# Dilated attention in near blocks and residues modulo 4, the two parts joined through DRAM

## The chip, the core and the metric

The kernel runs on one core of a Trainium2 chip. The metric is the device time of one execution in microseconds (us). The kernel before takes 1123.94 us, the median of three runs (1122.03 to 1125.61). The engines are TensorE (PE: matmuls and transposes; its weight loads are listed as PEld), VectorE (DVE), ScalarE (ACT), GpSimdE (POOL, which here issues most loads of the attention) and SyncE (SP, which issues the other DMAs).

## The reference, cut to what matters

One decoder layer on a sequence of 1024 tokens, width 1024. A projection of 10 pieces feeds two branches: attention with 8 heads of 64, and a gated recurrence. Gates merge them, and a last matmul and a norm end the layer. The change touches the attention alone. It is a mixture of three causal patterns, (window, dilation) = (128, 1), (512, 4) and (2048, 16):

```python
DILATED_PATTERNS = ((128, 1), (512, 4), (2048, 16))
...
    s = jnp.einsum('bdhnqe,bdhnke->bdhnqk', qs, ks) * (E ** -0.5) + bias[None, None, :, None]
    s = jnp.where(mask, s, NEG_INF)
    m = jnp.max(s, axis=-1, keepdims=True)
    p = jnp.exp(s - m)
    den = jnp.sum(p, axis=-1, keepdims=True)
    o = jnp.einsum('bdhnqk,bdhnke->bdhnqe', p, vs) / den
    lse = (m + jnp.log(den))[..., 0]
...
    w = jax.nn.softmax(jnp.stack(lses, 0), axis=0)
    return jnp.einsum('gbsh,gbshe->bshe', w, jnp.stack(outs, 0))
```

The three outputs are weighted with their denominators, so the mixture is a single softmax in which a key at distance delta counts as often as there are patterns that reach it: 0, 1, 2 or 3 times. A query sees every key up to a distance of 128, and beyond that only keys whose distance is a multiple of 4.

## The kernel before

All weights are split into a high and a low part of type float32r, and most products are three matmuls (high by high, low by high, high by low; mm3, lines 241 to 243). The projections form a **stream** of steps of 12 matmuls of 512 columns each. A step is prepared ahead of its product: DMA of the raw weights, ACT casts the high part (w_hi, line 248), DVE subtracts (w_lo, line 226, a helper that also makes ptl). Results leave the three banks m0 to m2 through ACT copies (line 329) and DVE additions (line 276).

The order of PE's instructions is written out by hand. In the attention stage pieces of attention stand between steps of the stream: `fill(amount)` runs as many quarters of a step as an amount times a rate comes to, so that the stream is spread over the stage. The other engines' orders come from a scheduler and are then fixed; each engine runs its queue in order.

Attention before, for each head h:

- load_head and load_half load queries (qp: both halves of the 128 partitions hold high and low parts), keys (k1, k2) and the biases by distance (toep, 1024 offsets); load_value loads values (vq), all on POOL's queue.
- score(h, i) makes the row of queries 128i to 128i+127 against all keys up to there, 128(i+1) wide, in chunks of at most 512 columns: two matmuls a chunk (lines 923 and 924), one DVE operation that adds the bias and takes the extreme (line 926), exp with its sum on ACT (line 929), a reciprocal (line 930) and the scaling (line 931). That is 36 blocks of 128x128 a head.
- turn(h, j, m, ...) transposes three or four blocks of a pair of rows on PE (line 941), and ACT and DVE split them (pth line 945, ptl).
- value(h, j, m, ...) multiplies them with the values (line 956), mostly 256 columns at a time, into one of two halves of a bank; at the end of a pair of rows the result goes out (lines 961 to 963).

The blocks of a row that no pattern needs in full (far keys at distances that are not multiples of 4) are computed and masked by a bias of -1e30.

Of the kernel before, what the change touches and what calls it, by code (L numbers as in the profile page):

```python
# [32 lines left out]
TOEP = 1152  # L33
# [6 lines left out]
def _consts():  # L40
    z = np.arange(TOEP)
    delta = z - (P - 1)
# [7 lines left out]
    for window, dilation in PATTERNS:  # L50
        count += (delta >= 0) & (delta <= window) & (delta % dilation == 0)
# [16 lines left out]
ATT_W = (2.6, 1.4, 0.9, 0.7)  # L68
# [111 lines left out]
def hybrid_layer(ctx: ExitStack, tc: tile.TileContext, x, w_ada, b_ada, w_in, w_branch_a, w_branch_b, w_out,  # L180
# [38 lines left out]
    vq_d = dram.tile([NH // 2, P, 8, 2, P], F32, name="vq_d")  # L219
# [222 lines left out]
    def ev_v(p, wait=2):  # L442
        def ev(src, th, psum):
            t = as_ct(src, psum)

            def turn():
# [3 lines left out]
                for n in (0, 2):  # L450
                    vs = ctile(F32R).rearrange("p (a h e) -> p a h e", a=2, h=2)
                    got = pt[:, n:n + 2].rearrange("p a (h e) -> p a h e", h=2)
                    nc.scalar.copy(vs[:, :, :, 0:E], got)
                    sub(vs[:, :, :, E:P], got, vs[:, :, :, 0:E])
                    nc.sync.dma_start(vq_d[p][:, 4 * th + n:4 * th + n + 2], vs.bitcast(F32))
                    last_v[p] = vs
# [61 lines left out]
    with ExitStack() as st:  # L518
# [184 lines left out]
        def bias_add(b):  # L703
            sl = slice(384 * b, 384 * b + 384)
            nc.vector.tensor_tensor(lc[:, sl], pbs[b], lc[:, sl], ALU.add)
            if b == 2:
                nc.gpsimd.dma_start(toep_d, lc)
# [79 lines left out]
        bias_row(2)  # L787
        bias_add(2)
# [79 lines left out]

    with ExitStack() as at:
# [4 lines left out]
        po2 = psO.tile([P, 2, 256], F32, name="po2")  # L874
        heads = {}

        def load_head(h):
            p = h // 2
            if p > 0:
                stream.need(f"qk{p}")  # L880
            while turned.get(("v", p)) != 2:
                stream.step()
            qp, k1, k2 = ([ap1.tile([P, 512], F32R, name=f"{n}{c}") for c in range(2)] for n in ("qp", "k1", "k2"))
            toep = ap1.tile([P, S], F32, name="toep")
            heads[h] = qp, k1, k2, toep, [None, None]
            load_half(h, 0)
            if h == 0:
                load_half(h, 1)
            load_value(h, 0)

        def load_half(h, c):


            qp, k1, k2, toep, _ = heads[h]
            if h == 0 and c == 1:
                got = last_v[0][:, 0, 0, 0:1].bitcast(F32)
                for t in (qp[1], k1[1], k2[1]):
                    nc.gpsimd.tensor_copy(t[:, 0:1], got)
                nc.gpsimd.tensor_copy(toep[:, 512:513], got)
            nc.gpsimd.dma_start(toep[:, half_of(c)],  # L900
                                bass.AP(tensor=toep_d.tensor, offset=toep_d.offset + h * TOEP + 512 * c,
                                        ap=[[1, P], [1, 512]]))
            p, r = h // 2, slice(E * (h % 2), E * (h % 2) + E)
            for dst, n in ((qp, 4 * p), (k1, 4 * p + 2), (k2, 4 * p + 3)):
                for hh in range(2):
                    nc.gpsimd.dma_start(dst[c][E * hh:E * hh + E],
                                        qk_d[n + hh if dst is qp else n][r, half_of(c)].bitcast(F32R))

        def load_value(h, n):
            vq = heads[h][4][n] = ap2.tile([P, 4, P], F32R, name="vq", bufs=3)  # L910
            nc.gpsimd.dma_start(vq, vq_d[h // 2][:, 4 * n:4 * n + 4, h % 2].bitcast(F32R))

        def score(h, i):
            qp, k1, k2, toep, _ = heads[h]
            kw = P * (i + 1)
            s = ap2.tile([P, (768, 1024)[i // 2 % 2]], F32, name=f"s{i // 2 % 2}")
            st2 = ap2.tile([P, 4], F32, name="st2", bufs=8)
            prev = 3.0e38
            for ks in range(0, kw, 512):
                w = min(512, kw - ks)  # L920
                ps = psS.tile([P, 512], F32, name="pss")
                q = qp[i // 4][:, i % 4 * P:i % 4 * P + P]
                nc.tensor.matmul(ps[:, :w], q, k1[ks // 512][:, :w], start=True, stop=False)  # L923
                nc.tensor.matmul(ps[:, :w], q, k2[ks // 512][:, :w], start=False, stop=True)  # L924
                x0, a = kw - ks - w, ks // 512
                nc.vector.tensor_tensor_reduce(s[:, ks:ks + w], ps[:, :w], toep[:, x0:x0 + w][:, ::-1], -1.0,  # L926
                                               prev, ALU.add, ALU.min, st2[:, a:a + 1])
                prev = st2[:, a:a + 1]
            nc.scalar.activation(s[:, :kw], s[:, :kw], AF.Exp, bias=prev, scale=-1.0, accum_out=st2[:, 2:3])  # L929
            nc.vector.reciprocal(st2[:, 3:4], st2[:, 2:3])  # L930
            nc.vector.tensor_scalar(s[:, :kw], s[:, :kw], st2[:, 3:4], None, ALU.mult)
            return s

        def turn(h, j, m, pn):
            pt = pools["t"].tile([P, 4, P], F32, name="pt").rearrange("p a b -> p (a b)")
            for kk in range(2):
                kt = 2 * m + kk
                for b in range(2):
                    if kt <= 2 * j + b:
                        c0 = kk * 256 + (b * P if kt <= 2 * j else 0)  # L940
                        nc.tensor.transpose(pt[:, c0:c0 + P], pn[b][:, kt * P:(kt + 1) * P], ident)  # L941
            w = 512 if m < j else 384
# [6 lines left out]
        def value(h, j, m, parts):  # L949
            vq, hh = heads[h][4], h % 2  # L950
            po = po2[:, j % 2]
            for kk in range(2):
                kt = 2 * m + kk
                c0, n = kk * 256, (256 if kt <= 2 * j else P)
                for a, src in enumerate(parts):
                    nc.tensor.matmul(po[:, 256 - n:256], vq[kt // 4][:, kt % 4], src[:, c0:c0 + n],  # L956
                                     start=kt == 0 and a == 0, stop=kt == 2 * j + 1 and a == 1)
            if m == j:
                t1 = ap1.tile([E, 256], F32, name="t1")
                oa = ap2.tile([E, 256], F32, name="oa")  # L960
                nc.scalar.copy(t1, po[E:2 * E])
                nc.vector.tensor_tensor(oa, po[0:E], t1, ALU.add)
                nc.sync.dma_start(oa_d[h // 2][E * hh:E * hh + E, 256 * j:256 * j + 256], oa)

        items = [(h, j) for h in range(NH) for j in range(4)]
        rows = {}

        def begin(n):

            if n < len(items):  # L970
                h, j = items[n]
                rows[n] = []
                for i in (2 * j, 2 * j + 1):
                    rows[n].append(score(h, i))
                    if i == 1:
                        if h > 0:
                            load_half(h, 1)
                        load_value(h, 1)
                    if i == 7 and h + 1 < NH:
                        load_head(h + 1)  # L980
                    yield
# [3 lines left out]
        def run_late(keep):  # L985
            while len(late) > keep:
                value(*late.pop(0))

        load_head(0)
        first = begin(0)  # L990
# [510 lines left out]
```

## Time and profile before

| | |
|---|---|
| median of the runs | 1123.94 us |
| the profiled execution's own time | 1122.96 us |
| its span | 1121.1 us |
| PE, DVE, ACT, POOL busy | 1095.0, 806.8, 555.2, 124.6 us |
| attention stage, on the span | 95 to 436 us |
| granted PE clock in it | 1.00 |
| mean DMA rate over the span | 169 GB/s |

The span runs from the first to the last instruction of the program; the time has 1.9 us more around it. In rows of groups, a line of the kernel, the engine, the operation and "output<-inputs" come first, then the shapes and the count, then busy us, mean ns of one, and the idle time of the engine ahead of them with what ended it. In a timeline the first two numbers are the start in the span and the duration, both in us. Durations of overlapping matmuls contain each other.

### The profile page before, as it was taken

What the parts mean: (1) busy time and instruction counts of PE and PEld (TensorE: products, weight loads), DVE (VectorE), ACT (ScalarE), POOL (GpSimd) and SP (SyncE); (2) the same over time, 40 slices, a digit from 0 to 9 for tenths busy, and PEclk for the clock granted to TensorE, in tenths of its full rate; (3) what the DMA queues carried; (4) which work ended last, traced back from release to release, by engine and by line L of the source; (5) the groups of instructions that cost most, each with busy time, mean ns of one, the idle gap of its engine ahead of it and who ended that gap; (6) DMA issues with size and microseconds to landing.
All of it is one profiled execution on the core that took longest, in us unless ns stands there. A gap on an engine that the chain in (4) does not pass through costs nothing.

```text
span 1121.1 us, 21828 instructions
## 1 busy us (share of the span) xinstructions
PE 1095.0 (98%) x8302; PEld 905.4 (81%) x8302; DVE 806.8 (72%) x1607; ACT 555.2 (50%) x1144; POOL 124.6 (11%) x207
## 2 busy tenths in 40 slices
PE   8999999999999999999999999989999999999997
PEld 6687888888888888778887788878887888887886
DVE  5587888878777876844879788887977772869053
ACT  5565656687555555622455554545554442334021
POOL 1112203203212201100000000000010012000000
PEclk9999999999999999999999999999999999999999
DMA  9849657736636625756625354353534389854052
GB/s 311 261 128 251 172 173 200 176 95 181 162 102 169 153 66 171 248 174 201 217 86 180 119 175 138 127 160 95 184 122 159 131 266 343 258 193 141 14 188 75
DMA packets 161608, 189.54 MB, mean 169 GB/s; under 512 B 11440, under 2 KB 107824, under 8 KB 161504
## 3 DMA queue, kind: packets, MB, share of 16 engines
q1 hardware_dynamic: 140080, 153.95, 42.6%
q0 software_dynamic: 21024, 33.60, 12.2%
q8 instruction: 65, 1.06, 0.4%
q10 hardware_dynamic: 400, 0.61, 0.2%
q14 instruction: 39, 0.32, 0.1%
HBM read 129.36 MB, written 58.76 MB: 168 GB/s over the span
## 4 chain that ended last, share of the span: by engine, by line
PE 78%; DVE 8%; issue 7%; DMA 3%; ACT 2%; POOL 1%; POOLq 0%; DVEq 0%; ACTq 0%
PE m L241 15%; PE m L243 15%; PE m L242 15%; PE pq L241 4%; PE pq L242 4%; PE pq L243 4%; PE po L956 2%; PE pt L941 2%; PE pp L1122 2%; PE pss L924 1%; PE pss L923 1%; DVE w_lo L226 1%; PE pou L1218 1%; PE pm L669 1%; PE pm L672 1%
## 5 line engine op out<-in xcount | busy, mean ns | idle before, releaser
L226 DVE TENSOR_TENSOR w_lo<-w_raw,w_hi 128x512 fp32r<-128x512 f32 x156 | 106.7, 686 | 61.2 <-ACT w_hi L248 60.7
L248 ACT CAST w_hi<-w_raw 128x512 fp32r<-128x512 f32 x146 | 90.5, 621 | 43.0 <-PE m L243 29.7
L248 ACT CAST w_hi<-w_s 128x512 fp32r<-128x512 f32 x90 | 55.9, 621 | 56.4 <-PE m L243 37.5
L329 ACT COPY ct<-m 128x512 f32<-128x512 f32 x90 | 52.6, 585 | 57.3 <-PE m L243 52.8
L276 DVE TENSOR_TENSOR ct<-m,ct 128x512 f32<-128x512 f32 x90 | 61.7, 686 | 24.4 <-PE m L243 24.1
L226 DVE TENSOR_TENSOR w_lo<-w_s,w_hi 128x512 fp32r<-128x512 f32 x90 | 61.7, 686 | 12.3 <-ACT w_hi L248 11.4
L929 ACT ACTIVATE s<-s,st 128x128 f32<-128x128 f32 (+3 forms) x64 | 49.8, 778 | 33.0 <-DVE st L926 33.0
L945 ACT CAST pth<-pt 128x512 fp32r<-128x512 f32 (+1 forms) x80 | 43.5, 544 | 34.0 <-PE pt L941 29.7
L1226 POOL TENSOR_TENSOR ssh<-ssh,halfh 128x4 f32<-128x4 f32 x16 | 19.5, 1216 | 335.2 <-DVE ssh L1225 335.2
L226 DVE TENSOR_TENSOR ptl<-pt,pth 128x512 fp32r<-128x512 f32 (+1 forms) x80 | 50.5, 631 | 7.4 <-ACT pth L945 6.6
L241 PE MATMUL m<-t4h,w_hi 128*128 128x512 f32 x120 | 49.5, 412 | 3.3 <-issue 1.9
L241 PE MATMUL m<-b11h,w_hi 128*128 128x512 f32 x124 | 50.8, 410 | 0.2 <-DVE ct L276 0.2
L241 PE MATMUL m<-b22h,w_hi 128*128 128x512 f32 x124 | 50.9, 410 | 0.0
L241 PE MATMUL m<-t3h,w_hi 128*128 128x512 f32 x120 | 49.5, 412 | 1.2 <-ACT w_hi L248 1.2
L241 PE MATMUL m<-b21h,w_hi 128*128 128x512 f32 x124 | 50.5, 408 | 0.0
L242 PE MATMUL m<-b22h,w_lo 128*128 128x512 f32 x124 | 48.5, 391 | 1.5 <-issue 1.5
L241 PE MATMUL m<-t2h,w_hi 128*128 128x512 f32 x120 | 49.2, 410 | 0.6 <-ACT ct L329 0.6
L241 PE MATMUL m<-t1h,w_hi 128*128 128x512 f32 x120 | 49.4, 412 | 0.3 <-DVE ct L276 0.3
L243 PE MATMUL m<-b11l,w_hi 128*128 128x512 f32 x124 | 48.6, 392 | 0.0
L243 PE MATMUL m<-b21l,w_hi 128*128 128x512 f32 x124 | 48.6, 392 | 0.0
L243 PE MATMUL m<-b22l,w_hi 128*128 128x512 f32 x124 | 48.6, 392 | 0.0
L242 PE MATMUL m<-b11h,w_lo 128*128 128x512 f32 x124 | 48.6, 392 | 0.0
(371 smaller groups left out, 3227.7 us busy)
## 6 DMA issues: line engine op xcount, KB each, us to landing
w_raw<-in_w_in_dram SPq DMA_DIRECT2D x128, 256.0 KB, 3.4
wa<-in_w_ada_dram SPq DMA_DIRECT2D x16, 512.0 KB, 9.4
qk_d<-ct SPq DMA_DIRECT2D x32, 256.0 KB, 3.2
k<-qk_d POOLq DMA_DIRECT2D x64, 128.0 KB, 5.2
toep<-toep_d POOLq DMA_DIRECT2D x16, 256.0 KB, 5.4
qp<-qk_d POOLq DMA_DIRECT2D x32, 128.0 KB, 4.9
vq_d<-ct SPq DMA_DIRECT2D x16, 256.0 KB, 3.8
vq<-vq_d POOLq DMA_DIRECT2D x16, 256.0 KB, 4.1
```

What stands on the lines that cost most here:

```text
L226: nc.vector.tensor_tensor(out_, a, hi.bitcast(F32), ALU.subtract)
L241: nc.tensor.matmul(ps, ah, bh, start=start, stop=False, skip_group_check=more)
L242: nc.tensor.matmul(ps, al, bh, start=False, stop=False, skip_group_check=more)
L243: nc.tensor.matmul(ps, ah, bl, start=False, stop=stop, skip_group_check=more)
L248: nc.scalar.copy(hi, src)
L276: nc.vector.tensor_tensor(out_, a, b_, op)
L329: nc.scalar.copy(c[name], b[which])
L929: nc.scalar.activation(s[:, :kw], s[:, :kw], AF.Exp, bias=prev, scale=-1.0, accum_out=st2[:, 2:3])
L941: nc.tensor.transpose(pt[:, c0:c0 + P], pn[b][:, kt * P:(kt + 1) * P], ident)
L945: nc.scalar.copy(pth[:, :w], pt[:, :w])
L956: nc.tensor.matmul(po[:, 256 - n:256], vq[kt // 4][:, kt % 4], src[:, c0:c0 + n], start=kt == 0 and a == 0, stop=kt == 2 * j + 1 and a == 1)
L1122: nc.tensor.matmul(to[:, 0], k_[:, o:o + 32], q_[:, o:o + 32], start=True, stop=True)
```

## The change

A query row's keys are divided in two parts. The **near** part of a block of 128 queries is its own and the previous key block: 15 blocks a head. The **far** part takes queries and keys by residue modulo 4, since beyond a distance of 128 only multiples of 4 count: for each half r of the sequence (512 queries) and each residue n, 128 queries against the keys of that residue, 128 in the first half and 256 in the second: 12 blocks a head, so 27 in all. Two bias tables (384 offsets each) replace the one of 1152, and the bias of the near table is -1e30 beyond a distance of 128, that of the far table up to there.

An item is now (h, r) with 8 rows: 4 near and 4 far. Each row has its own maximum (kept negated, so a minimum) and sum; they stand in `stats`, near ones by position, far ones by residue. As the two orders put a query on different partitions, `weigh` writes both to DRAM (SP) and reads each in the other's order (POOL), then finds the common maximum and the factor of each row's scaling. `normal` scales rows by it ahead of their transposes. Value products of both parts add up in one bank of 512 columns, ordered by residue, for which near products read the transposed weights with a step of 4. Far values are loaded by residue. Scores run 14 rows ahead of the first transposes.

```diff
@@ dilated attention: tables and loads @@
-TOEP = 1152
+HALF_T = 384
+TOEP = 2 * HALF_T
...
-    vq_d = dram.tile([NH // 2, P, 8, 2, P], F32, name="vq_d")
+    vq_d = dram.tile([NH // 2, 8, P, 2, P], F32, name="vq_d")
+    ex_d = dram.tile([2 * NH, 2, 512, 2], F32, name="ex_d")
...
+            if part == "n":
+                src = vq_d[p][4 * n:4 * n + 4, :, h % 2].rearrange("a p e -> p a e")
+            else:
+                src = vq_d[p].rearrange("j (a c) h e -> (j a) c h e", c=4)[P * n:P * n + P, :, h % 2]
@@ score @@
-            for ks in range(0, kw, 512):
...
+            if part == "n":
+                i = 4 * r + n
+                q = qps[h, r][:, P * n:P * n + P]
+                keys = [(b // 4, slice(P * (b % 4), P * (b % 4) + P)) for b in range(max(i - 1, 0), i + 1)]
+                if len(keys) == 2 and keys[0][0] == keys[1][0]:
+                    keys = [(r, slice(P * n - P, P * n + P))]
+            else:
+                q = qps[h, r][:, n::4]
+                keys = [(c, slice(n, None, 4)) for c in range(r + 1)]
...
+            for c, sl in keys:
+                k1, k2 = k1s[h, c][:, sl], k2s[h, c][:, sl]
+                m = k1.shape[1]
+                nc.tensor.matmul(ps[:, w:w + m], q, k1, start=True, stop=False)
+                nc.tensor.matmul(ps[:, w:w + m], q, k2, start=False, stop=True)
+                w += m
+            s = ap1.tile([P, w], F32, name=f"s{r}{part}{n}")
+            nc.vector.tensor_tensor_reduce(s, ps[:, :w], bias[h][part == "f"][:, :w][:, ::-1], -1.0, 3.0e38,
+                                           ALU.add, ALU.min, st[:, 0:1])
+            nc.scalar.activation(s, s, AF.Exp, bias=st[:, 0:1], scale=-1.0, accum_out=st[:, 1:2])
+        def weigh(h, r):
+            st, ex = stats.pop((h, r)), ex_d[2 * h + r]
+            nc.sync.dma_start(ex[0].rearrange("(n p) m -> p n m", p=P), st[:, 0, 0:4])
+            nc.sync.dma_start(ex[1].rearrange("(p n) m -> p n m", n=4), st[:, 0, 4:8])
+            nc.gpsimd.dma_start(st[:, 1, 0:4], ex[1].rearrange("(n p) m -> p n m", p=P))
+            nc.gpsimd.dma_start(st[:, 1, 4:8], ex[0].rearrange("(p n) m -> p n m", n=4))
+            f = ap2.tile([P, 2, 8], F32, name="f")
+            g = ap2.tile([P, 8], F32, name="g")
+            nc.vector.tensor_tensor(g, st[:, 0, :, 0], st[:, 1, :, 0], ALU.min)
+            nc.vector.tensor_tensor(f, g.unsqueeze(1).to_broadcast([P, 2, 8]), st[:, :, :, 0], ALU.subtract)
+            nc.scalar.activation(f, f, AF.Exp)
+            nc.vector.tensor_tensor(st[:, :, :, 1], st[:, :, :, 1], f, ALU.mult)
+            nc.vector.tensor_tensor(g, st[:, 0, :, 1], st[:, 1, :, 1], ALU.add)
+            nc.vector.reciprocal(g, g)
+            nc.vector.tensor_tensor(g, g, f[:, 0], ALU.mult)
@@ value @@
+                    if blocks:
+                        to = to.rearrange("p (c x) -> p c x", c=4)[:, :, 32 * at_:32 * (at_ + blocks)]
+                        to = to.rearrange("p c (g a) -> p c g a", g=blocks)
+                        got = got.rearrange("p (g a c) -> p c g a", g=blocks, c=4)
+                    else:
+                        to = to[:, P * at_:P * at_ + P]
@@ the order of the work @@
-ATT_W = (2.6, 1.4, 0.9, 0.7)
+        PLAN = ((2, 1, 2), (3, 2, 3, 3))
+        GROUP_W, ROW_W = ((0.9, 0.9, 0.8), (0.6, 0.6, 0.6, 0.6)), 0.12
```

PLAN says how many rows are scored beside each of the three or four groups of transposes of an item; GROUP_W and ROW_W are the amounts of stream work beside a group and a row. In the numbers of the changed kernel, lines 941 and 942 are the score matmuls, 945 the bias and minimum, 959 to 965 the joining on DVE, 976 the scaling, 1009 the transposes, 1033 the value products and 1042 the sum of the halves of the output; 230 and 245 to 247 are before's 226 and 241 to 243.

More of the change, by code (lines that the diff above doesn't have):

```diff
@@ L881, in load_head, with load_value @@
+        def load_value(h, part, n):
+            p = h // 2
             while turned.get(("v", p)) != 2:
                 stream.step()
[L883 to L918, printed above, removed]
-            for ks in range(0, kw, 512):
[L920 to L932, printed above, removed]
@@ L934, in turn @@
-        def turn(h, j, m, pn):
-            pt = pools["t"].tile([P, 4, P], F32, name="pt").rearrange("p a b -> p (a b)")
[L936 to L942, printed above, removed]
+            t = values[h, part, n] = ap1.tile([P, 4, P], F32R, name=f"v{part}{n}")
@@ L947, in turn @@
             return pth, ptl
[L949 to L981, printed above, removed]
+        banks_o = {}
@@ new lines, in all_rows @@
+        def all_rows():
+            for h in range(NH):
+                for r in range(2):
+                    for part in ("nf", "fn")[r]:
+                        for n in range(4):
+                            score(h, r, part, n)
+                            if r == 1 and part == "n" and h + 1 < NH:
+                                if n == 0:
+                                    load_half(h + 1, 0)
+                                if n == 3:
+                                    load_half(h + 1, 1)
+                            if n == 3 and part == "fn"[r]:
+                                weigh(h, r)
+                            yield
@@ L986, in run_late @@
             while len(late) > keep:
[L987 to L1012 removed]
+                late.pop(0)()
@@ new lines, in hybrid_layer, with rows_of, finish_item, go @@
+        PLAN = ((2, 1, 2), (3, 2, 3, 3))
+        GROUP_W, ROW_W = ((0.9, 0.9, 0.8), (0.6, 0.6, 0.6, 0.6)), 0.12
+        scores = all_rows()
+        def rows_of(n, w):
+            for _ in range(n):
+                next(scores, None)
+                fill(w)
+        def finish_item(h, r, products, parts, last, loads):
+            def go():
+                value(h, r, products, parts, last)
+                for part, n in loads:
+                    if h + 1 < NH:
+                        load_value(h + 1, part, n)
+            return go
```

149 lines of the change are left out of this document (117 added, 32 removed).

## The prediction

> **What bounds the kernel now.** I read the page's busy times first, then the table of stretches, to find the stage that the change touches, then who waits for whom in that stage, and last the timeline of TensorE (PE) alone, since that is where the cost of a small matmul can be read.
>
> ```profile
> PE 1095.0 (98%) x8302; PEld 905.4 (81%) x8302; DVE 806.8 (72%) x1607; ACT 555.2 (50%) x1144; POOL 124.6 (11%) x207
> 95.00:436.00 341.00, 338.62 (x1822) 285.63 (x1821) 270.41 (x633) 206.23 (x413) 66.27 (x113) 1.00 0.59 154
> PE m L241 <- ACT w_hi L248: 1.2, 1, 1.2
> ...
> PE m L242 <- DVE w_lo L226: 0.2, 1, 0.2
> ```
>
> The second row is the attention stage, 95 to 436 us: its length, then busy us of PE, weight loads, DVE, ACT and POOL, the granted clock, the DMA share and GB/s. PE works for 338.6 of 341 us at full clock, and its four kinds of waits there come to 2.2 us (first and last shown). Attention is interleaved with projection matmuls of the stream, so there is always something to run. The stage therefore lasts as long as the sum of what its PE instructions occupy. A change to attention is worth what it takes off that sum, less any new wait. DVE is next, with 71 us idle.
>
> "Busy" of overlapped matmuls is not what they occupy; the distance from start to start is.
>
> ```profile
> 201.18 0.39 PE L923 MATMUL pss<-k,qp 128*128 128x512 f32 x1
> 201.41 0.39 PE L924 MATMUL pss<-k,qp 128*128 128x512 f32 x1
> 201.64 0.28 PE L923 MATMUL pss<-k,qp 128*128 128x256 f32 x1
> 201.75 0.28 PE L924 MATMUL pss<-k,qp 128*128 128x256 f32 x1
> 201.87 0.28 PE L956 MATMUL po<-pth,vq 128*128 128x256 f32 x1
> 201.99 0.28 PE L956 MATMUL po<-ptl,vq 128*128 128x256 f32 x1
> 202.11 0.22 PE L956 MATMUL po<-pth,vq 128*128 128x128 f32 x1
> 202.17 0.28 PE L956 MATMUL po<-ptl,vq 128*128 128x128 f32 x1
> 202.29 0.44 PE L241 MATMUL m<-t4h,w_hi 128*128 128x512 f32 x1
> 202.57 0.40 PE L242 MATMUL m<-t4h,w_lo 128*128 128x512 f32 x1
> ...
> 203.04 0.49 PE L941 MATMUL pt<-kc,s 128*128 128x128 f32 x3
> 203.28 0.48 PE L241 MATMUL m<-t4h,w_hi 128*128 128x512 f32 x1
> 203.60 0.39 PE L242 MATMUL m<-t4h,w_lo 128*128 128x512 f32 x1
> 208.20 0.34 PE L923 MATMUL pss<-k,qp 128*128 128x384 f32 x1
> 208.37 0.34 PE L924 MATMUL pss<-k,qp 128*128 128x384 f32 x1
> 208.55 0.39 PE L241 MATMUL m<-t2h,w_hi 128*128 128x512 f32 x1
> ```
>
> 512 columns take 0.23 us (201.18 to 201.41), 384 take 0.175 (208.20 to 208.55 by two), 256 take 0.1175 (201.64 to 202.11 by four). The two of 128 columns look cheap, 0.06 and 0.12, but the 512-wide one behind them then takes 0.28 where 0.23 is usual: from 202.11 to 202.57, less 0.23, is 0.23 for two, **0.115 each**. So 128 columns cost what 256 do: the time is that of the 128 weights loaded for each matmul. Likewise three transposes take 203.04 to 203.60 less 0.23, that is 0.11 each.
>
> **The change part by part.**
>
> *Matmuls and transposes.* Counts of before, eight heads:
>
> ```profile
> L923 PE MATMUL pss<-k,qp x96: 221/392/497, 95.4 to 415.6; 128*128 128x512 f32 x48, 128*128 128x128 f32 x16, 128*128 128x256 f32 x16, 128*128 128x384 f32 x16
> L956 PE MATMUL po<-pth,vq x160: 220/279/388, 118.2 to 435.4; 128*128 128x256 f32 x128, 128*128 128x128 f32 x32
> L941 PE MATMUL pt<-kc,s 128*128 128x128 f32 x288 | 44.8, 273 | 0.4 <-DVE s L931 0.3
> ```
>
> Each is doubled (L924 and the ptl half). A head before has 12 scores of 512, 4 of 384, 4 of 256 and 4 of 128: 12x0.23 + 4x0.175 + 4x0.1175 + 4x0.115 = 4.39 us; 32 value products of 256 and 8 of 128: 4.68; 36 transposes: 3.96. Sum 13.03 us.
>
> After, from the code: near scores are 6 rows of 256, one row of 128 and row 4 of each head in two halves of 128; far scores are 4 rows of 128 and 4 rows of two times 128. Doubled, that is 12 of 256 and 30 of 128: 12x0.1175 + 30x0.115 = 4.86. Values: 6 near keys serve two query blocks, 3 serve one, and 12 far products are 128 wide: again 12 and 30, 4.86. Transposes: 27, 2.97. Sum 12.69 us. The difference is 0.34 us a head, **-2.7 us** for eight. By columns alone 9 blocks of 36 would have been 26 us. They go because the scores rise from 24 matmuls to 42, nearly all too narrow to hide their weights. On PE one row (queries 512 to 639 of a head) before:
>
> ```order
> L923 MATMUL pss<-k_3761,qp_3760 128x512
> L924 MATMUL pss<-k_3763,qp_3760 128x512
> L923 MATMUL pss<-k_3762,qp_3760 128x128
> L924 MATMUL pss<-k_3764,qp_3760 128x128
> L241 MATMUL m_3807<-t3h,w_hi 128x512
> ```
>
> and after, the last near row of one item, then value products (pth is read as 4x32 or 4x64), among the stream's:
>
> ```order
> L941 MATMUL pss<-k_2334,qp_2333 128x256
> L942 MATMUL pss<-k_2335,qp_2333 128x256
> L245 MATMUL m_2298<-t4h,w_hi 128x512
> L246 MATMUL m_2298<-t4h,w_lo 128x512
> L247 MATMUL m_2298<-t4l,w_hi 128x512
> L1033 MATMUL po<-pth,vn_2278 128x4x32
> L1033 MATMUL po<-ptl,vn_2278 128x4x32
> L1033 MATMUL po<-pth,vn_2376 128x4x32
> L1033 MATMUL po<-ptl,vn_2376 128x4x32
> L1033 MATMUL po<-pth,vn_2376 128x4x64
> L1033 MATMUL po<-ptl,vn_2376 128x4x64
> ```
>
> The 512-wide scores are gone, and the values have become streams of short pieces.
>
> *Strided operands.* Residues are taken with a step of 4 floats: far scores read keys and queries so, and near values read pth and ptl so (12 of 256, 6 of 128 a head). No PE operand of before is strided. Lower bound: no cost, the 256-wide row's 0.1175. Upper bound: a strided read spans four times as many bytes, so 256 columns cost as two 512-wide rows, 0.46, and 128 as one, 0.23: 12x0.34 + 30x0.115 = 7.5 us a head, 60 us. I take half pace, 0.23 for 256 columns: the one slower moving operand that the trace has, the plain fp32 of the transposes, goes at 0.11 for 128 columns, half the 256-wide row's pace (though its weights may account for that). Then 128-wide products stay hidden under their weights and the price is 12x(0.23-0.1175)x8 = **+10.8 us**. [...]
>
> *DVE and ACT.* Groups of the stage before, then the forms that remain:
>
> ```profile
> L226 DVE TENSOR_TENSOR ptl<-pt,pth 128x512 fp32r<-128x512 f32 (+1 forms) x80 | 50.5, 631 | 7.4 <-ACT pth L945 6.6
> L926 DVE CUSTOM_DVE_ANT_0 s<-pss,toep 128x512 f32<-128x512 f32 (+2 forms) x64 | 36.9, 583 | 12.1 <-PE pss L924 12.1
> L931 DVE TENSOR_SCALAR s<-s,st 128x128 f32<-128x128 f32 (+3 forms) x64 | 33.3, 520 | 1.2
> L926 DVE CUSTOM_DVE_ANT_0 s<-pss,toep,st 128x128 f32<-128x128 f32 (+3 forms) x32 | 17.4, 543 | 0.6
> L930 DVE RECIPROCAL st<-st 128x1 f32<-128x1 f32 x64 | 10.2, 159 | 11.8 <-ACT s L929 11.7
> L926 DVE CUSTOM_DVE_ANT_0 s<-pss,toep 128x256 f32<-128x256 f32 x8 | 3.3, 409 | 0.0
> L931 DVE TENSOR_SCALAR s<-s,st 128x256 f32<-128x256 f32 x8 | 2.8, 352 | 0.2
> L929 ACT ACTIVATE s<-s,st 128x256 f32<-128x256 f32 x8 | 4.0, 506 | 3.0 <-DVE st L926 3.0
> ```
>
> Before, the first five come to 148 us. After, 56 turns of 0.63 are 35; 128 maxima of at most 0.41 are 52; 128 scalings of at most 0.35 are 45; 192 small operations of the joining at 0.16 are 31: 163 us at most, 15 more, out of 71 idle. ACT has 135 us idle. At nothing, as long as nothing is queued behind a wait.
>
> *The join.* That is the new wait. Each of 16 items sends its maxima and sums to DRAM (SP), reads the other part's (POOL), and then L959 on DVE. Eight-byte pieces add 16x1280 = 20480 packets, a tenth or so of what there is, to a DMA share of 0.59: taken at nothing.
>
> ```profile
> oa_d<-oa SPq DMA_DIRECT2D x32, 64.0 KB, 3.4
> vq<-vq_d POOLq DMA_DIRECT2D x16, 256.0 KB, 4.1
> k<-qk_d POOLq DMA_DIRECT2D x64, 128.0 KB, 5.2
> 228.94 0.69 DVE L226 TENSOR_TENSOR w_lo<-w_s,w_hi 128x512 fp32r<-128x512 f32 x1
> 237.32 0.39 PE L241 MATMUL m<-b22h,w_hi 128*128 128x512 f32 x1
> ```
>
> From the last exp (0.7 with its sum), a small write (3.4) and a read (4.1), the result is there after about 8.2 us. On DVE, from the last maximum of an item whose near part comes first:
>
> ```order
> L945 ISA s0f_3116,stats<-pss,bias_2766 128x128
> L945 ISA stats 128x1
> L410 TENSOR_TENSOR ct<-m_2645,ct 128x512
> L230 TENSOR_TENSOR w_lo<-w_raw_2484,w_hi 128x512
> L230 TENSOR_TENSOR ptl<-pt,pth 128x512
> L959 TENSOR_TENSOR g<-stats 128x8
> L960 TENSOR_TENSOR f<-g,stats 128x16
> L945 ISA s1f_3181,stats<-pss,bias_2766 128x256
> ```
>
> L959 stands three operations of 0.69 behind it, 2.1 us of work, 2.6 at DVE's share of 79%. So DVE stands still for some 5.6 us, eight times; where the far part comes first there lie about 5 us of work between and it waits perhaps 2. That is about 60 us of DVE's 71 idle, and queued behind are the next maxima, w_lo and ptl of the stream. What covers it for PE: the split of a step's weights is made 8.4 us before its product (228.94 to 237.32 above: this w_s is the sum of prep_s4, whose product is the one with b22). Bounds: nothing, and all 60 us. I take near nothing, since 5.6 is less than 8.4: PE's waits of 2.2 us double, **+2.2 us**. Key loads are issued behind joins on POOL, but a first use comes 36 stream matmuls (8.3 us) after the last use of the old, against 5.2 and some issues ahead: covered, by little. If that cover fails, PE waits at the first score of a head for what is missing.
>
> *The rest.* The output bank is now one for a whole item, where two halves took turns; the next item's first product waits until it is copied out.
>
> ```profile
> L962 DVE TENSOR_TENSOR oa<-po,t 64x256 f32<-64x256 f32 x31 | 12.8, 412 | 4.0 <-ACT t L961 4.0
> L961 ACT COPY t<-po 64x256 f32<-64x256 f32 x31 | 11.5, 370 | 18.0 <-PE po L956 17.8
> ```
>
> Two copies and two adds are 1.6 us; 18 stream matmuls, 4.1 us, and four transposes lie between: nothing. If the adds stand behind the join, this belongs to the rival below. In the start one bias product and its addition go (768 offsets for 1152), on no path that the stage of attention sees: nothing.
>
> Sum: 1122.96 us of the profiled execution (span 1121.1) - 2.7 + 10.8 + 2.2 = 1133.3; it lies 1.0 us below the median of the three runs, so 1134.
>
> **The rivals.**
>
> *Strided reads are free.* Then 1123.9 - 2.7 + 0 to 2.2 is 1121 to 1123. For it: the weight loads already hide half of a 256-wide stream; against: no row shows a strided read at full pace.
>
> *Narrow matmuls are cheaper.* If the delay behind two 128-wide ones is paid once in a run of many, each costs the mean of 0.06 and 0.115, 0.0875: 48 more of them a head save a further 48x0.0275x8 = 10.6 us, and with free strides 1111. Against: the 0.28 behind the pair. [...]
>
> *The join stops PE.* ACT's exps wait for DVE's maxima, and bank copies stand behind them on ACT. The cover is then not 8.4 us but one step of the stream, 12x0.23 = 2.8 us. Once the wait exceeds it, PE pays the rest: 8x(5.6-2.8) = 22 us, 1156. For it: in-order queues; against: DVE that runs late waits less.
>
> *Strides cost four times.* 1123.9 - 2.7 + 60 + 2.2 = 1183. [...]
>
> **How the numbers follow.** Chances: forecast 0.40, free strides 0.24, the join stops PE 0.16, cheap narrow matmuls 0.10, fourfold strides 0.10. Leaving out the last two, the range goes from 1117 (4 us below free strides, as narrow matmuls may cost a little less than one pair shows) to 1160 (a little above the join's 1156). A measurement of this kernel can tell 0.3%, 3.4 us, from no change. Faster: the narrow rival and a little under half of free strides, 0.20. Same: the rest of free strides, 0.14. Slower: 0.66. The forecast's own range is 1128 to 1140.
>
> **What would show it.** In the profile after, the attention stage should have PE as full as now, pairs of far scores 0.115 apart, transposes x216, and near values of 256 columns 0.23 apart. If these stand 0.12 apart, free strides are right; 0.46, the fourfold rival. Many 128-wide matmuls in a row at under 0.1 show the narrow rival. PE waits on w_lo, pt or m that end at DVE behind L959, adding up to over 10 us, show the join. The forecast is wrong if the stage is shorter than 338 us.

## The result and the profile after

The changed kernel takes 1234.53 us, the median of four runs (1230.07 to 1237.87), beside 1122.99 us for the kernel before: a ratio of 1.0993 [1.0964, 1.1021]. Forecast was 1134 us, with a range up to 1160. The profiled execution took 1237.82 us, its span is 1236.1 us.

From the page of the kernel after, the busy times of the engines:

```profile
PE 1161.0 (94%) x8388; PEld 961.1 (78%) x8388; DVE 800.6 (65%) x1742; ACT 571.5 (46%) x1270; POOL 154.8 (13%) x254
```

From the table of stretches, the attention stage, now 95 to 557 us (columns as in the row of before, 95 to 436):

```profile
95.00:557.00 462.00, 410.11 (x1928) 345.35 (x1927) 266.38 (x773) 223.51 (x541) 99.91 (x167) 0.92 0.52 121
```

The stage is 121 us longer, and that is more than the whole loss; what follows it takes a little less than before. PE (TensorE) is idle for 52 us of it where it was idle for 2.4, and the granted clock is 0.92 where it was 1.00. DVE (VectorE) and ACT do about as much as before. So PE waits, and it also works more slowly. Who it waits for, in the waits of PE (all three kinds) and of DVE at the join (total, times, longest, in us):

```profile
PE pss L941 <- DVE stats L945: 42.4, 33, 4.4
PE pt L1009 <- DVE s1f L976: 5.4, 4, 2.3
PE pt L453 <- DVE ct L230: 3.9, 1, 3.9
```

```profile
DVE g L959 <- DMA stats<-ex_d: 39.4, 13, 6.0
DVE g L959 <- issue: 12.9, 2, 7.1
```

DVE stands at the join (L959) for 52 us by these two rows, 57 with a last one of 4.8 that is put down to another transfer: in sum the 60 us foreseen. The two kinds of items stand the other way round than foreseen, though. One join of each kind, the far part last (foreseen 5.6) and the near part last (foreseen 2):

```profile
504.37 0.17 DVE L959 TENSOR_TENSOR g<-stats 128x8 f32<-128x8 f32 x1 [1.41 <-DMA stats<-ex_d]
...
531.45 0.17 DVE L959 TENSOR_TENSOR g<-stats 128x8 f32<-128x8 f32 x1 [4.26 <-DMA stats<-ex_d]
```

The eight joins with the far part last stand 14 us in all, the eight with the near part last 43. PE's three kinds of waits come to 51.7 of the 52 us idle, so the loads that are queued behind the joins on POOL cost PE nothing here. The promised sign, waits on pt behind DVE, is there with 9.3 us, just short of the 10 that were to show the join. But most of the wait is not on w_lo, pt or m. It is at the first matmul of a score row, for the statistics of an earlier row. The timeline shows what kind of wait that is:

```profile
290.43 0.28 PE L942 MATMUL pss<-k,qp 128*128 128x128 f32 x1
...
290.75 0.42 DVE L945 CUSTOM_DVE_ANT_0 s1n<-pss,bias 128x256 f32<-128x256 f32 x1 [0.29 <-PE pss L942]
...
291.09 0.08 DVE L945 DVE_READ_ACCUMULATOR2_ANT stats<- 128x1 f32 x1
...
291.23 0.38 PE L941 MATMUL pss<-k,qp 128*128 128x256 f32 x1 [0.52 <-DVE stats L945]
```

PE ends a row (290.43 and its 0.28), DVE takes its minimum, and only then PE begins the next row, although that row goes into the other half of the bank: `pair_s` puts two rows in one bank, and the kernel's waits guard the bank as a whole. By the order of the rows in the code, all 33 of these waits, 42.4 us, stand at the second row of a bank. Why the waits guard the whole is not shown: the code makes each of these banks as one tile, so the runs can't tell a guard by bank from a guard by tile.

The other promised signs, in the timeline of PE at a granted clock of 1.00. Near values of 256 columns, then far scores, then far values:

```profile
292.72 0.42 PE L1033 MATMUL po<-pth,vn 128*128 128x256 f32 x1
292.95 0.42 PE L1033 MATMUL po<-ptl,vn 128*128 128x256 f32 x1
293.18 0.42 PE L245 MATMUL m<-t4h,w_hi 128*128 128x512 f32 x1
```

```profile
506.99 0.40 PE L942 MATMUL pss<-k,qp 128*128 128x128 f32 x1
507.20 0.42 PE L941 MATMUL pss<-k,qp 128*128 128x128 f32 x1
507.43 0.41 PE L942 MATMUL pss<-k,qp 128*128 128x128 f32 x1
507.66 0.43 PE L245 MATMUL m<-t3h,w_hi 128*128 128x512 f32 x1
...
508.46 0.28 PE L1033 MATMUL po<-ptl,vf 128*128 128x128 f32 x1
...
509.13 0.27 PE L1033 MATMUL po<-ptl,vf 128*128 128x128 f32 x1
```

Near values stand 0.23 apart: half pace, as forecast. Far values, 128 columns read in a row, stand 0.112 apart (508.46 to 509.13 by six): no cheaper in a long run, so the narrow rival falls. But the far scores shown, also 128 columns, stand 0.21 to 0.23 apart where 0.115 was forecast.

### The profile page after: what moved, and what is told of

It reads as the page before. It is cut to its first block, busy times and chain, and to the rows that moved or that the text cites. A ratio compares the mean times of both kernels' runs of the same rounds, so it can differ in the third digit from the quotient of the medians.

```text
span 1236.1 us, 22426 instructions
## 1 busy us (share of the span) xinstructions
PE 1161.0 (94%) x8388; PEld 961.1 (78%) x8388; DVE 800.6 (65%) x1742; ACT 571.5 (46%) x1270; POOL 154.8 (13%) x254
## 4 chain that ended last, share of the span: by engine, by line
PE 59%; DMA 14%; DVE 14%; issue 6%; ACT 5%; POOL 2%; SPq 0%; POOLq 0%; DVEq 0%; ACTq 0%
PE m L245 12%; PE m L246 11%; PE m L247 11%; DMA ex_d<-stats 5%; DMA stats<-ex_d 3%; PE po L1033 3%; PE pq L245 2%; PE pq L247 2%; PE pq L246 2%; DVE w_lo L230 2%; PE pss L941 2%; PE pp L1221 2%; PE pss L942 1%; DMA ld<-in_w_ada_dram 1%; DVE ct L280 1%
## 5 line engine op out<-in xcount | busy, mean ns | idle before, releaser
L941 PE MATMUL pss<-k,qp 128*128 128x128 f32 (+1 forms) x168 | 57.9, 347 | 42.5 <-DVE stats L945 42.4
L941 PEld LDWEIGHTS pss<-k,qp 128*128 128x128 f32 x168 | 44.4, 265 | 58.1 <-DVE stats L945 54.1
L942 PE MATMUL pss<-k,qp 128*128 128x128 f32 (+1 forms) x168 | 59.4, 356 | 0.0
L245 PE MATMUL m<-t1h,w_hi 128*128 128x512 f32 x120 | 52.3, 436 | 0.2 <-DVE ct L280 0.2
L245 PE MATMUL m<-b11h,w_hi 128*128 128x512 f32 x124 | 51.7, 417 | 0.0
L230 DVE TENSOR_TENSOR ptl<-pt,pth 128x512 fp32r<-128x512 f32 (+1 forms) x56 | 37.4, 668 | 21.5 <-ACT pth L1012 21.3
L246 PE MATMUL m<-b21h,w_lo 128*128 128x512 f32 x124 | 50.2, 405 | 0.0
```

Source lines behind the costliest of these rows:

```text
L230: nc.vector.tensor_tensor(out_, a, hi.bitcast(F32), ALU.subtract)
L245: nc.tensor.matmul(ps, ah, bh, start=start, stop=False, skip_group_check=more)
L246: nc.tensor.matmul(ps, al, bh, start=False, stop=False, skip_group_check=more)
L941: nc.tensor.matmul(ps[:, w:w + m], q, k1, start=True, stop=False)
L942: nc.tensor.matmul(ps[:, w:w + m], q, k2, start=False, stop=True)
```

## The experiments

The theory that the experiments start from: three costs. Two rows share a score bank; DVE stands at the join ahead of the minima that free those banks; strided operands. Rivals: the join alone is the cause and the banks only show where its wait lands; or strides are most of it.

**Each cost undone, alone and together.** A bank for each row:

```diff
-            if n % 2 == 0:
-                pair_s[0] = psS.tile([P, 2, 256], F32, name="pss")
-            ps, w = pair_s[0][:, n % 2], 0
+            ps, w = psS.tile([P, 512], F32, name="pss"), 0
```

> Edit: every score row takes a bank of its own (128x512) in place of half of one that it shares with the next row; everything else as after. Bank theory: in the profile after, PE's waits in the attention stage end at the bias-and-minimum of DVE (L941 on stats, 42.4 us on PE and 54.1 us on its loads), because the second row of a pair goes to the bank that DVE still reads; the idle time of 52 us then also lowers the granted clock (0.92). With own banks PE's idle time falls below 15 us, the clock returns to 0.98 or more, and the time falls from 1234 to 1160 or less. Join theory: PE idles because DVE stands at the join (L959); the same waits remain, now for the row two before, and the time stays above 1215. Stride theory (strided reads cost nearly all of it): above 1225.

Without the exchange, each part weighed with its own statistics:

```diff
-            nc.sync.dma_start(ex[0].rearrange("(n p) m -> p n m", p=P), st[:, 0, 0:4])
...
-            nc.gpsimd.dma_start(st[:, 1, 4:8], ex[0].rearrange("(p n) m -> p n m", n=4))
+            nc.gpsimd.tensor_copy(st[:, 1], st[:, 0])
```

> Edit: the four DMAs of a join are left out, and a copy on POOL puts each part's own maxima and sums in place of the other part's (so the parts are weighted wrongly); all other work remains. Join theory: DVE no longer stands at L959 (57 us in after), PE's idle time falls from 52 us to below 15 and the time to 1165 or less. Bank theory: the wait on the shared bank remains, only a little shorter since DVE is less late; 1200 to 1230. Stride theory: above 1225.

Without strides (`flat`), the work the same but on other elements:

```diff
-                q = qps[h, r][:, n::4]
-                keys = [(c, slice(n, None, 4)) for c in range(r + 1)]
+                q = qps[h, r][:, P * n:P * n + P]
+                keys = [(c, slice(P * n, P * n + P)) for c in range(r + 1)]
...
-                        got = got.rearrange("p (g a c) -> p c g a", g=blocks, c=4)
+                        got = got.rearrange("p (g c a) -> p c g a", g=blocks, c=4)
```

> Edit: contiguous operands alone; shared banks and the exchange stay. If PE were bound by its own instructions, 33 us less than 1234.5, 1200. If PE's speed in this stage is set by DVE's answers, part of what the strides free becomes waiting, and less is gained: 1205 to 1225.

And these edits together, the names telling which:

> Edit: own banks and no exchange; strided operands stay. Against the kernel with contiguous operands as well (1135.6) this prices the strides alone, with PE otherwise nearly undisturbed. Stride theory with both parts (near values 256 columns at 0.23 in place of 0.1175, and far scores 0.233 each in place of 0.115 because their weights are strided): 10.8 + 192x0.118 = 33 us more, 1165 to 1172. Stride theory as on record (near values alone): 1144 to 1150. If the two stalls were additive and independent (-40 and -51 from 1234.5): 1143.

> Edit: own banks and contiguous operands; the exchange stays. Against 1135.6 this prices the join alone. Join theory in the size on record (22 us and the clock it costs): 1155 to 1165. If the join only hurts through the shared bank: 1135 to 1142. Against own banks alone (1194.6) it should be 30 to 36 us less if strides cost 33 us, 11 to 15 less if they cost 10.8.

> Edit: own banks, no exchange, and contiguous operands in place of those with a step of 4 (far queries and keys by blocks, near values from contiguous columns; so other scores and sums are computed, in the same numbers of instructions and columns). All theories agree that what is left is the count of PE instructions: 2.7 us below before by the sum on record, so 1118 to 1126. If it is far above, a fourth cause is missing; if it is below 1112, 128-wide matmuls in a run are cheaper than 0.115.

| undone | us | to before |
|---|---|---|
| nothing | 1234.53 | 1.0993 [1.0964, 1.1021] |
| strides | 1216.96 | 1.0830 [1.0734, 1.0925] |
| shared bank | 1194.58 | 1.0639 [1.0590, 1.0688] |
| exchange | 1183.62 | 1.0541 [1.0511, 1.0572] |
| shared bank, strides | 1196.86 | 1.0651 [1.0620, 1.0682] |
| shared bank, exchange | 1149.95 | 1.0233 [1.0204, 1.0263] |
| all three | 1135.55 | 1.0113 [1.0084, 1.0143] |

All three are real, and they don't add up: the bank costs 40 us with the exchange and 34 without, strides 18 us in the changed kernel (7 to 29 by the intervals), nothing clear once the banks are apart (1196.86 for 1194.58), and 14 when the exchange is gone too. A bank for each row and no exchange each landed between what the theories gave, so neither is the whole cause; `own_flat` (expected at least 11 us below `own_bank`) and `own_flat_noex` (at most 1126 expected) were misses. The numbers fit a PE that pays the later of its own work and DVE's answer. Waits of PE in the two versions that undo the bank or the exchange alone, one row each:

```profile
PE pss L939 <- DVE stats L943: 20.7, 13, 5.7
```

```profile
PE pss L941 <- DVE stats L945: 21.9, 29, 1.9
```

With banks apart there are few waits and long ones (13, up to 5.7 us: the join). Without the exchange there are many short ones (29, at most 1.9 us: the pair, for all 29 stand at the second row of a bank). With all three undone 10.8 us remain at the score banks, which hold two rows; with four rows in them, further down, 0.2 remain:

```profile
PE pss L939 <- DVE stats L943: 10.8, 18, 2.8
```

**The joining on DVE put later**, behind the statistics of the third next row, in the changed kernel and with a bank for each row:

```diff
+            joins[h, r] = [st, 0, None]
...
+        def join(h, r):
...
+            st, _, later = joins.pop((h, r))
...
+            if later is not None:
+                nc.vector.tensor_copy(g[:, 0:1], later[:, 0:1])
             nc.vector.tensor_tensor(g, st[:, 0, :, 0], st[:, 1, :, 0], ALU.min)
...
+            if (h, r) in joins:
+                join(h, r)
```

> Edit: the DVE half of the join is put behind the third score row after it (by a one-column copy of that row's minimum into g), so its results have landed when DVE comes to it; the exchange and the shared banks stay. Join theory: as without the exchange, 1165 or less. Bank theory: DVE's wait at L959 goes, but PE still idles at the second row of a pair; 1200 to 1230. If the scaling then comes too late, transposes (L1009) wait for it, and the time is above 1234.

> Edit: own banks, and the DVE half of the join behind the third score row after it; nothing left out. If the join costs by holding DVE's queue and not by its results coming late, this is as without the exchange: within 8 us of the kernel with own banks and no exchange. If the data themselves come late (transposes waiting for scaling), 1180 to 1195, little better than own banks alone (1194.6). Either way it does not come near 1123.

1200.13 us, 1.0688 [1.0657, 1.0719], and with own banks 1174.94 us, 1.0456 [1.0401, 1.0511]: 34 and 20 us come back, less than the 51 and 45 that leaving the exchange out is worth. In `join_later` DVE's stand at the exchange falls to 8.5 us; PE's wait at the second rows of the banks is still 26.0 us, and its wait for scaled rows rises from 5.4 to 10.9 us. With own banks too (`own_join_later`) the stand falls to 11.3 us, and PE waits 6.2 us for banks (20.7 in `own_bank`) but 16.1 for scaled rows (7.3): part of the wait moves.

**Which stride makes the far scores slow.** Queries (the weights of the matmul) or keys (its moving operand) in a row, with own banks and no exchange:

> The kernel with own score banks and without the exchange (1149.95 us), with the far scores' queries, which are the weights of these matmuls, taken from 128 columns in a row in place of every fourth; the keys keep their step of 4. It computes the far scores of other queries. In the trace of 1149.95 the 240 far-score matmuls of 128 columns stand 0.228 us apart behind each other (second product) and 0.157 (first), 46.3 us in all, where 0.113 each would be 27.1. Theory 'strided weights': the weight load is what doubles; they fall to about 0.113 and the time to 1131 to 1142 (its floor is the version with no strides at all, 1135.55, less what near values cost there). Theory 'strided stream': the keys' step doubles them; the time stays at 1146 to 1152.

> The mirror of the run before: own score banks, no exchange, and the far scores' keys, the moving operand, taken from 128 columns in a row, while the queries, the weights, keep their step of 4. It computes far scores against other keys. 'Strided weights': 1146 to 1152 and still about 0.23 us from one matmul to the next. 'Strided stream': 1131 to 1142, and about 0.113. If both runs fall by about a half, both operands cost.

Weight loads of the second score product, min, median and max in ns: with both strides (`own_noex`), queries in a row, keys in a row:

```profile
L940 PEld LDWEIGHTS pss<-k,qp x168: 187/310/331, 97.0 to 434.1; 128*128 128x128 f32 x168
```

```profile
L940 PEld LDWEIGHTS pss<-k,qp x168: 187/189/338, 96.1 to 431.4; 128*128 128x128 f32 x168
```

```profile
L940 PEld LDWEIGHTS pss<-k,qp x168: 187/309/334, 98.1 to 433.1; 128*128 128x128 f32 x168
```

It is the weights: 0.31 us for 0.19, and the keys' step adds nothing to that. The second products go from 0.22 apart (median) to 0.12 with queries in a row, and stay at 0.23 with keys in a row. The time, however, is 1148.21 us, 1.0209 [1.0143, 1.0275], and 1148.39 us, 1.0210 [1.0150, 1.0270]: neither moved by 2 us (the intervals leave some 8), so my 1131 to 1142 for queries in a row was a miss. PE's waits for score banks rose from 4.6 to 10.9 us, and the clock fell from 0.998 to 0.990. The price has to be taken where PE doesn't wait.

**Exchange in 32-byte pieces**, banks apart, parts weighed with factors of other queries:

```diff
-            nc.sync.dma_start(ex[0].rearrange("(n p) m -> p n m", p=P), st[:, 0, 0:4])
+            nc.sync.dma_start(ex[0].rearrange("(p n) m -> p n m", n=4), st[:, 0, 0:4])
...
-            nc.gpsimd.dma_start(st[:, 1, 0:4], ex[1].rearrange("(n p) m -> p n m", p=P))
+            nc.gpsimd.dma_start(st[:, 1, 0:4], ex[1].rearrange("(p n) m -> p n m", n=4))
```

> The kernel with own score banks (1194.58 us), with the exchange written and read in 32-byte pieces on both sides: the same four transfers and the same waits, but not one 8-byte piece. It weighs parts with the factors of other queries. The 8-byte write lands after 5.4 us (median), the 32-byte one after 2.6; the two reads hardly differ (2.8 and 2.7). Theory 'small pieces': eight of the joins end with the near part, whose write is the one in 8-byte pieces, so 8 times 2.8 = 22 us go at most: 1172 to 1182. Theory 'round trip': DVE stands at the join because a write and a read follow each other at all, and the 2.8 us are mostly waited elsewhere: 1187 to 1196.

1172.38 us, 1.0424 [1.0356, 1.0491]: 22 us less, the size that small pieces were given. The edit widens the near part's write and the far part's read, the two transfers in 8-byte pieces. The write, before (`own_bank`) and with this edit:

```profile
DMA to landing us min/median/max: 3.2/5.1/9.3
```

```profile
DMA to landing us min/median/max: 1.4/2.8/6.3
```

The read's median goes from 2.8 to 2.6 us only, and DVE's stand at the join from 59 to 32 us.

**Both rows of a bank ahead of both minima.** The bank stays shared; PE writes it twice, then DVE reads it twice:

```diff
+            waiting.append((ps, w, st, f"s{r}{part}{n}", bias[h][part == "f"], (h, r, part, n)))
+            if n % 2:
+                for job in waiting:
+                    extreme(*job)
+                waiting.clear()
```

> The changed kernel (1234.53 us), with the bias and minimum of both rows of a score bank put behind the matmuls of both, so that the second row needn't wait until DVE has read the first. Two banks then hold four rows. Theory 'shared bank': what the changed kernel loses there is the wait inside a pair; it goes, and with twice the rows in flight this is at or below the version with a bank for each row: 1165 to 1195. Rival 'answers': PE is paced by how soon DVE answers at all, behind the join; a bank of two rows then comes free later than a bank of one, and the time is 1195 to 1235.

1180.70 us, 1.0497 [1.0412, 1.0583], 54 us less, by an order of instructions alone. Waits of PE in it, the first two of seven rows, then DVE's longest:

```profile
PE pt L1017 <- DVE s1f L984: 11.6, 5, 3.8
PE pt L1017 <- DVE s0n L984: 6.2, 1, 6.2
```

```profile
DVE g L967 <- DMA stats<-ex_d: 69.7, 15, 8.6
```

No wait for score banks is left. DVE stands longer at the join than in the changed kernel, yet PE pays less: four rows fit into the two banks, and of PE's waits 17.8 us are for scaled rows that come late; the next is 5.6 at L453, also behind DVE.

**The ladder, with PE kept full**: paired, without the exchange, and strides put back one kind at a time.

> The paired kernel (1180.70 us) without the exchange and with no strided operand in scores and near values: queries and keys of far scores and the transposed near weights are read in a row. The parts are weighed with their own statistics on both sides and the far scores are those of other queries and keys, so that only the work is the same. Theory 'three costs and no more': bank, exchange and strides are gone, TensorE is as full as in the kernel before, and only the count of matmuls is left: 1123 - 2.7 = 1120, between 1117 and 1125. Rival 'something else': own banks without exchange and strides took 1135.55, and if the 12.6 us above the kernel before were not the score banks' answers, this stays at 1130 to 1136.

> As the run before, but near values keep their step of 4 (0.23 us for 256 columns where 0.1175 is usual). Far scores are those of other queries and keys, parts are weighed with their own statistics. If TensorE is full, the 96 products cost what the prediction put them at, 10.8 us more than the run before: 1131 (1128 to 1135). If TensorE waits elsewhere, less than 5 us more.

> The paired kernel without the exchange, with all strides as the change has them; parts are weighed with their own statistics. Theory 'strided weights cost in full once TensorE is full': the 240 far-score matmuls of 128 columns stand some 0.19 us apart where 0.113 would do, 46.3 - 27.1 = 19 us more than the run before: 1150 (1145 to 1153). If far strides are hidden behind DVE's answers here as they were with own banks (1148.21 for 1149.95): within 4 us of the run before.

| | us | to before | step |
|---|---|---|---|
| no exchange, no strides | 1125.26 | 1.0024 [1.0002, 1.0045] | |
| near values strided | 1132.05 | 1.0079 [1.0051, 1.0108] | +6.8 |
| far scores strided too | 1149.48 | 1.0220 [1.0149, 1.0292] | +17.4 |
| exchange too | 1180.70 | 1.0497 [1.0412, 1.0583] | +31.2 |
| minima between the rows of a bank (the change) | 1234.53 | 1.0993 [1.0964, 1.1021] | +53.8 |

The intervals leave some 4, 9, 13 and 10 us either way in the four differences. The first row is what is left of count and covers. Its stage, and its waits of PE beside those for m:

```profile
95.00:446.00 351.00, 345.44 (x1935) 295.79 (x1935) 263.57 (x775) 218.52 (x542) 81.39 (x150) 0.98 0.65 159
```

```profile
PE po L1038 <- issue: 3.3, 1, 3.3
...
PE po L1038 <- DVE oa L1047: 2.0, 1, 2.0
```

The first wait, which the view gives to no one, ends at 252.71, 0.1 us after the last addition of the item before out of the same bank (252.19 and its 0.42). So some 5 us of waits are at the output bank, costed at nothing, against the 2.7 us that the count saves. That fits the 2.3 us above the kernel before, but no run took the output bank away.

**Paired, and the joining later.**

> The whole computation: rows paired as in the paired kernel (1180.70 us), and the joining on DVE put behind the third next row's statistics, so that DVE doesn't stand at the exchange while it is due for maxima. In the paired kernel DVE stands 76 us at the join and TensorE waits 18 us for scaled rows and none for score banks. Theory 'DVE's stand is what PE pays': with the stand gone it comes to 1152 to 1166, a few us above the version without the exchange. Rival 'the row is due': the scaled rows are due for their transposes when the exchange has barely come back, so the wait only moves from the maxima to the scaling, as with own banks (1174.94): 1168 to 1182.

1180.38 us, 1.0495 [1.0406, 1.0584]: no gain on 1180.70, though the intervals leave some 14 us either way. In its waits the scaled rows are late by as much as without the edit, and DVE still stands at the join:

```profile
PE pt L1030 <- DVE s1f L997: 11.5, 6, 3.5
PE pt L1030 <- DVE s0n L997: 6.4, 2, 5.5
```

```profile
DVE g L978 <- DMA stats<-ex_d: 46.3, 8, 7.2
DVE g L978 <- issue: 7.1, 1, 7.1
```

The edit took away only a third of the stand, 53 us of 76 being left: the joins with the near part last stand nearly as before (48 us for 53). So this run doesn't show what the stand costs once banks don't bind. That the due time of the scaled rows binds then is likely from `own_join_later`, where 11 us of the stand were left and PE waited 16 for scaled rows; it is not shown here.

**The exchange's pieces, paired.** The edit of `own_wide` in the paired kernel, and a version that computes everything, with the near statistics written row by row:

```diff
-            nc.sync.dma_start(ex[0].rearrange("(n p) m -> p n m", p=P), st[:, 0, 0:4])
...
+            if part == "n":
+                nc.sync.dma_start(ex_d[2 * h + r][0, P * n:P * n + P], st)
```

> The paired kernel (1180.70 us) with the exchange in 32-byte pieces on both sides; parts are weighed with the factors of other queries. Without the exchange the paired kernel takes 1149.48, so the exchange costs 31.2 there. Theory 'small pieces': the 8-byte write of the near part stands last in eight items and takes 2.8 us longer than the other; 8 times 2.8 is 22 of the 31: 1157 to 1164. Theory 'round trip': a write and a read behind each other cost most of it: 1170 to 1181.

> The whole computation: the paired kernel with the near part's statistics written to DRAM row by row, each as soon as the row's sum is there (64 writes of 128 pieces of 8 bytes in place of 16 of 512), so that only the last row's 128 pieces are left when the item is complete. 'Small pieces': the last write then lands about as soon as the 32-byte one (2.6 us for 5.4), and the time is near that of the run with 32-byte pieces: 1157 to 1168. 'Per transfer': a transfer of 8-byte pieces takes its 5 us whatever their count, or the further writes hold up the loads behind them on their queue: 1174 to 1190.

1157.05 us, 1.0306 [1.0276, 1.0336], for the 32-byte pieces: 23.7 of the exchange's 31.2 us are its 8-byte pieces. The write's median falls from 5.5 to 2.9 us, the read's from 3.1 to 2.4, so most of it should be the write. But row by row takes 1194.47 us, 1.0640 [1.0609, 1.0671], 14 us more than paired. Its DMA issues (count, KB each, median us to landing):

```profile
ex_d<-stats SPq DMA_DIRECT2D x64, 1.0 KB, 5.3
```

128 pieces of 8 bytes land no sooner than 512 did (5.5 in the paired kernel), so the last one should be as late as before; and PE now meets 6.2 us at the values' loads. Why a few small pieces take 5 us is open: one piece a row against four in line was not separated from their size. No version tried that computes everything beats the kernel before; the three best, own banks with the later joining (1174.94) and paired without and with it (1180.70, 1180.38), can't be told apart by their intervals.

## Why the prediction was wrong

The direction was right; the size was off by 100 us, and the time lies above the range and above even the fourfold rival.

- **Count, -2.7**: the durations hold (0.112 a narrow matmul), the narrow rival falls. Against its gain stand some 5 us of waits at the output bank, "nothing" in the prediction.
- **Strided near values, +10.8**: right in mechanism (0.23 apart), 6.8 in time; the intervals of the two runs leave some 2 to 11.
- **Strided far scores, nothing**: wrong. "128-wide products stay hidden under their weights" held for the keys, but the queries are the weights and are strided too; their load takes 0.31 for 0.19 us. +17.4 where PE is full.
- **The join, +2.2: the step that failed.** DVE's stand was foreseen in sum (60, measured 57), partly by luck: 45 and 16 were given to the two kinds of items, 14 and 43 were measured. The prediction gave every small write the 3.4 us of a 64 KB one; measured are 2.6 for the far part and 5.4 for the near part, whose 8-byte pieces were "taken at nothing"; wider pieces, in that write and the far part's read, took away 22 and 24 us in two versions. The prediction also named the next maxima among what is queued behind the join. But the cover, "5.6 is less than 8.4", was taken from one customer, w_lo of the stream. The score rows have no such lead: PE can go on only as far as there are score banks, two, and the changed code lets one row be in each at a time. The join stops PE in earnest, in the changed kernel through those banks: leaving the exchange out is worth 51 us there, and 31 with rows paired, where PE waits for scaled rows instead. The join rival had the right direction but put the wait in the stream's step, at 22 us.
- **The shared score bank: not in the prediction.** It costs 34 to 54 us, depending on what else is undone. The line that makes it stands in the changed code, not in the quoted diff; the row to ask was who frees a bank, and how many rows are in flight.
- **"PE as full as now"** was therefore false (52 us idle), and with the idle time the clock fell (0.92 for 1.00), which no term held.

## What to carry to other kernels

A wait of one engine is covered by the shortest lead among all that is queued behind it (here that of the score rows, not the 8.4 us of w_lo: without the exchange the changed kernel takes 51 us less), so list every customer with its own lead, and count the buffers, before setting a cost at nothing. Two results in one PSUM bank made writer and reader take turns here (33 waits, 42.4 us); write both, then read both: in this kernel that alone is 54 us. Price strides where the engine is full: in a stage that waits they look free (1196.86 us without them for 1194.58 with them, banks apart and the exchange in place), and their price comes back when the wait is mended (6.8 and 17.4 us, rows paired and no exchange).

## What the hardware showed besides

*The clock was lower where PE had stood idle.* Stretches of 40 us of the changed kernel, then the same of the paired one (length, PE busy first, the clock third from the end):

```profile
420.00:460.00 40.00, 33.61 (x146) 28.62 (x145) 21.12 (x69) 14.69 (x39) 4.53 (x8) 0.83 0.32 82
460.00:500.00 40.00, 35.74 (x175) 29.76 (x174) 22.75 (x66) 18.07 (x48) 9.22 (x16) 0.96 0.56 115
```

```profile
420.00:460.00 40.00, 36.22 (x181) 31.43 (x180) 23.66 (x74) 16.10 (x43) 4.54 (x7) 0.91 0.53 106
460.00:500.00 40.00, 40.00 (x215) 33.90 (x214) 25.30 (x60) 20.55 (x45) 2.78 (x4) 1.00 0.39 89
```

In the three of these stretches in which PE is idle for 3.8 to 6.4 of 40 us, the clock is 0.83 to 0.96; in the one without idle time it is 1.00. Shorter stretches show what is in such a mean, here the 3.41 us ahead of a fall of the clock and the fall itself:

```profile
429.74:433.15 3.41, 0.69 (x4) 0.52 (x4) 2.91 (x8) 1.07 (x4) 0.00 (x0) 1.00 0.39 133
433.15:439.98 6.83, 6.83 (x24) 5.85 (x24) 1.74 (x5) 2.36 (x7) 0.55 (x1) 0.50 0.09 11
```

The clock is halved for 6.83 us while PE is busy all the time, and 512-wide matmuls of the stream then stand 0.43 apart for 0.23 (437.60 to 438.03). It is halved again from 450.22 to 457.05 in the first stretch, from 491.18 to 494.59 in the second and from 434.29 to 441.12 in the third: 13.7, 3.4 and 6.8 us of 40 at half speed make 0.83, 0.96 and 0.91. Over the stage of the changed kernel 0.08 of 462 us is 37 us' worth of clock. That the idle time causes it was not tried by itself; every edit that took waits away raised the clock (0.965 over the whole run, 0.983 paired, 0.994 without the exchange too). The four stretches at half speed last 3.41 us or twice that, and in the 3.41 us ahead of them PE was idle for 2.7, 1.3, 1.8 and 2.1 us, in none of them all the time.

*A strided weight load* (step of 4 floats, 128 columns) took 0.31 us for 0.19 (medians of L940 in `own_noex` and `own_noex_flat_q`), and a 128-wide matmul behind another such one then cost 0.23 us (507.20 to 507.43 in the changed kernel) for 0.115 before. *A strided moving operand* of 256 columns (the same step) also cost 0.23 (292.72 to 292.95) for 0.1175 before; of 128 columns it cost nothing more (0.12 in `own_noex_flat_q`, where only the keys keep their step).
